# Attention block on one core: low parts of the queries among zeros in full-height tiles, second half of the values behind the convolution's projections, layer norm one step later

## The chip, the cores and the metric

The kernel runs on one core of a Trainium2 chip. A core has a matrix engine (TensorE, PE in the profile, whose weight loads are shown apart as PEld), three engines for elementwise work (VectorE, DVE; ScalarE, ACT; GpSimd, POOL) and a queue engine that issues most transfers (SyncE, SP). Each engine takes its instructions in the order in which they are written for it and waits on semaphores for the others. The metric is the device time of one execution in microseconds.

## The reference, cut to what matters

The program is two transformer blocks, one behind the other. The change lies in the first block, in its attention and convolution branches:

```python
z = rms_norm(x) @ w_in                      # convolution, queries, keys, values, gates
a, gate = split(u)                          # convolution branch
y = a * sigmoid(gate)
y = depthwise_conv(y, 31 taps) + dw_b       # over 1024 tokens
y = silu(layer_norm(y))
# attention branch: 4 heads, two components of 64 features each
s = einsum("bqhcd,bkhcd->bhcqk", q, k) * 64 ** -0.5
p = softmax(where(causal, s, -inf))
a = p[:, :, 0] - lam * p[:, :, 1]           # lam: one number, from four rows of 64
o = rms_norm(einsum("bhqk,bkhe->bqhe", a, v)) * (1 - lam_init)
merged = gates[0] * (conv_out @ w_conv) + gates[1] * (o @ w_attn)
```

A mixture of experts and the second block follow; nothing in them is changed.

## The kernel before

There are 1024 tokens, 1024 features and 128 partitions, so 8 token tiles and 8 feature blocks. Every product of float32 operands is made of three: each operand is split into a high and a low part (`split`, lines 83 to 89: ScalarE makes the high part on L85, VectorE or GpSimd the low one on L86), and `mm3` (L118 to L120) adds high by high, high by low and low by high. `K.weng` names the engine of L86 for weights; during the convolution's projections and the first gates it is GpSimd. Weights come through three buffers for what is loaded and three pairs for what is split.

`phase_a` runs in this order on TensorE: the values, in two halves of 256 columns (each half: 8 token tiles of 24 products, 128x256, into the PSUM tiles PT, copied out by ScalarE on L326); `lambda_a` (the number `lam`: four tiny loads, L275, L276, an Exp on L277, a product on L281) and `consts_b`; the convolution's projections, 8 pairs of 24 + 24 products 128x512 into the banks PB, joined on VectorE on L343; 16 blocks of `gates(0)`, 24 products each; then the queries and keys in eight groups of 96 products 128x256 into PT.

The 31 taps of the convolution (L346, L348) are 124 VectorE instructions over 1024 tokens. They are given a low priority, and the scheduler puts them among VectorE's other work, in the order in which their inputs come; no other large work stands between them.

Each group of queries and keys is normed (ScalarE square, VectorE L428, L132, GpSimd L133, VectorE L431 into `qn`) and turned by transposes one group later (`flip`: `q_T` on L403, `k_T` on L411, whose results VectorE and ScalarE write on L414 and L415). Among the groups stand four steps of the layer norm of the convolution, set by the list `steps`: `ln_mean` (sums over channels on TensorE, L368, then GpSimd and ScalarE) and `ln_rest` (sums of squares on L376, the square root, the gain, the silu).

In the attention loop each of 8 token tiles has 4 heads, and each head two components. A component's scores are made of two products per 512 keys: L472 has the query's high part twice, above itself, against the keys' high and low parts (128 rows of the array), and L473 the query's low part against the keys' high part (64 rows). L475 adds the mask. VectorE takes the maximum (L477), ScalarE the exponential (L480), VectorE joins the components (L488), TensorE transposes (L494), ScalarE copies (L495), TensorE multiplies with the values (L497). `q_parts` (L451 to L453) prepares the parts of two heads. The score tiles are PT, two of them. Into the attention's waits the scheduler puts the products of the other half of the gates (`gates(1)`, L118 to L120 into PB).

Of the kernel before, what the change touches and what calls it, by code (L numbers as in the profile page):

```python
# [19 lines left out]
P = 128  # L20
T = 1024
# [4 lines left out]
CB = 96  # tokens of an expert in a block  # L26
# [8 lines left out]
class Ring:  # L35
    """Buffers taken in turn."""
# [21 lines left out]
def arena(K, pool):  # L58
    """SBUF: slots of [128, 1024], each a line of tiles that follow one another."""

    def new(i, dt=F32):
        return pool.tile([P, 1024], dt, name=nm(f"s{i}"), tag=f"slot{i}")

    K.N = lambda *ii: [new(i) for i in ii]
    K.NR = lambda *ii: [new(i, F32R) for i in ii]
    K.NP = lambda *pp: Ring([(new(a, F32R), new(b, F32R)) for a, b in pp])
# [14 lines left out]
def split(K, src, hi, lo, scale=None, eng=None):  # L81
    """hi + lo = src * scale, both exact in float32r."""
# [9 lines left out]
def split4(K, src, dst):  # L92
    """src [4, 512]: high parts on rows 0 to 3 of dst, low parts on rows 32 to 35, zeros between."""
# [17 lines left out]
def wunit(K, src, kt, n):  # L111
    """src [kt*128, n], loaded and split: views [128, kt, n]."""
    return wsplit(K, wload(K, src, kt, n), kt, n)
# [9 lines left out]
def fm_block(K, u, ps, rh, rl, kt=KD):  # L123
    """Feature-major product: weights stationary, tokens moving."""
# [4 lines left out]
def rstd_pool(K, out, ss, n, scale, eps):  # L129
    """out = (ss * scale + eps) ** -0.5 on [128, n]."""  # L130
# [5 lines left out]
def sig(K, out, src, scale=0.5, bias=None):  # L136
    """sigmoid through tanh, which shares a table with exp."""
# [25 lines left out]
def load_rows(K, specs, buf, ps, engs):  # L163
    """specs: list of (key, AP [r, 128]); per-partition columns: K.cols[key] = AP [128, r]. Returns the step past the loads."""
# [27 lines left out]
def bcast(ap, n, p=P):  # L192
    """A row of n elements in DRAM, on p partitions."""
# [3 lines left out]
def row_rstd(K, x, junk, tag):  # L197
    """(mean square + eps) ** -0.5 of the rows of a token tile."""
# [12 lines left out]
def grow(K, slot, ap, eng=None):  # L211
    """A gain over the features, on all partitions."""
# [5 lines left out]
def norm(K, x, xn, junk, g, tag):  # L218
    """Rms norm of a token tile times g."""
# [11 lines left out]
def turn(K, xn, his, los, j, banks):  # L231
    """A token tile, transposed, split: into tile j of his, los (4 slots each: pairs of feature blocks, 512 tokens)."""
# [34 lines left out]
def lambda_a(K, I, buf):  # L267
    """lambda, and half the gain of the heads' norms with its factor."""
# [19 lines left out]
def phase_a(K, I, gd, cvd, on_out, on_x2):  # L288
# [29 lines left out]
    # values, on tokens  # L318
    V = [kn(s, 2) for s in N(28, 29, 30, 31)]
    rows_a(K, I)  # L320
    for n in range(2):
        us = us if n == 0 else tm_units(2048 + n * 256)
# [4 lines left out]

    lambda_a(K, I, tr())
    consts_b(K, I, tr())

    # convolution branch: gated projections (doubled; the taps are halved), then the taps
# [18 lines left out]
    def gates(q, banks):  # L350
        """Of half the tokens, to DRAM; less 1, doubled: the branches are halved."""
# [7 lines left out]

    gates(0, dn)  # L360
    # layer norm of the convolution over channels, twice its silu: in steps among the queries and keys
# [24 lines left out]
    steps = [[(ln_mean, 0)], [], [(ln_rest, 0)], [(ln_mean, 1)], [], [(ln_rest, 1)], [], []]  # L386

    # queries and keys: on tokens, normed, transposed; the scale goes with the queries.
    # q, a tile pair a slot: [component, head * 128 + token]. A component of the keys of a head has
    # a slot of its own, high and low parts above one another (the high part at the component's rows).  # L390
# [49 lines left out]
    # attention; its normed output, transposed: a tile pair a slot  # L440
    oT = N(0, 1, 2, 3)
    qdr = Ring((46, 47))

    def q_parts(i, hp):
        """Of a pair of heads: the high part of a component twice above itself; the low parts."""
        q = qT[i // 2][:, i % 2 * 512 + hp * 256 : i % 2 * 512 + (hp + 1) * 256]
        qd = NR(qdr())[0]
        ql = qd[:, 512:768]
        for c in range(2):
            r, o, h = comp[c], comp[1 - c], qd[:, c * 256 : (c + 1) * 256]  # L450
            nc.scalar.activation(h[r], q[r], AF.Copy)  # L451
            nc.scalar.activation(h[o], q[r], AF.Copy)
            nc.vector.tensor_tensor(ql[r], q[r], h[r].bitcast(F32), op=ALU.subtract)  # L453
        return qd, ql
# [3 lines left out]
    for i in range(NT):  # L458
        nk = (i + 1) * P
        r0 = K.small.tile([P, 4], F32, name=nm("r0"), tag="r0")  # L460
        for h in range(4):
            if h % 2 == 0:
                qd, ql = q_parts(i, h // 2)
# [1683 lines left out]
```

## Time and profile before

| | |
|---|---|
| runs | 3045.42 us median of 3 (3037.07 to 3050.23) |
| profiled execution | span 3048.1 us; the page gives no other time for it |
| PE busy | 2885.1 us, 95% |
| DVE, ACT, POOL busy | 1941.2, 1361.3, 388.6 us |
| 261.5 to 291.5 us | PE busy 3.63 of 30.00 us |
| 426.5 to 603.6 us (attention) | PE busy 175.85 of 177.10 us |

The stretch that the change touches is the first 605 us or so of the span. A time of the page is counted from the span's start. A busy PE is not a PE at its peak: the matmuls are pipelined, and how fast it goes is read from the distance between the starts of two of them.

### The profile page before, as it was taken

Reading aid. Unit: us, or ns where it says so; the run is one execution under the profiler, and the core shown is the slowest. Engines: PE = TensorE matmul, PEld = TensorE weight load, DVE = VectorE, ACT = ScalarE, POOL = GpSimd, SP = SyncE. Lnnn points to the kernel's source line nnn. Section 1 sums busy time; section 2 is a strip of 40 time slices with the busy share of each in tenths; the row PEclk is TensorE's granted clock in tenths of the full one; section 3 lists DMA queues with packets and bytes.
Section 4 is the critical chain, followed back from the end, with each engine's and each line's share of the span. In section 5 each row is a group of like instructions: output and inputs, shape, how many; then the busy total and the mean of one; then the engine's idle time right before and its main releaser. Section 6 shows DMA issues by size and latency. Waiting matters only on the chain.

```text
span 3048.1 us, 41828 instructions
## 1 busy us (share of the span) xinstructions
PE 2885.1 (95%) x15803; PEld 2287.3 (75%) x15803; DVE 1941.2 (64%) x3245; ACT 1361.3 (45%) x2274; POOL 388.6 (13%) x288
## 2 busy tenths in 40 slices
PE   8996999999979999899799999999899999999998
PEld 7875866787767777777576766777677788888886
DVE  3798476645779998789663554435755565555555
ACT  4121466622458887677432335213456433242222
POOL 2252410000021110110231222210100000000000
PEclk9997989999989999999889989889899999999999
DMA  4141111276589999899741423214343342353332
GB/s 130 48 127 54 35 39 42 80 231 198 203 293 378 372 368 333 300 376 365 247 134 53 113 68 88 68 55 142 106 109 89 95 131 90 97 165 96 92 104 97
DMA packets 365226, 473.29 MB, mean 155 GB/s; under 512 B 36744, under 2 KB 224661, under 8 KB 365020
## 3 DMA queue, kind: packets, MB, share of 16 engines
q1 hardware_dynamic: 357708, 453.26, 45.3%
q0 software_dynamic: 7168, 16.79, 1.7%
q8 instruction: 125, 2.05, 0.3%
q14 instruction: 81, 0.66, 0.1%
q10 hardware_dynamic: 144, 0.52, 0.1%
HBM read 420.65 MB, written 59.02 MB: 157 GB/s over the span
## 4 chain that ended last, share of the span: by engine, by line
PE 44%; DVE 4%; DMA 1%; POOL 1%; ACT 1%; issue 1%; SPq 0%; POOLq 0%; DVEq 0%; ACTq 0%
PE PC L118 11%; PE PC L119 11%; PE PC L120 11%; PE PC L1335 1%; PE PC L1778 1%; PE PC L1442 1%; PE PC L1295 1%; PE PC L1441 1%; PE PC L1772 1%; DMA s<-y2d 0%; PE PC L1424 0%; PE PC L1752 0%; PE PC L1422 0%; PE PC L237 0%; PE PC L1662 0%
## 5 line engine op out<-in xcount | busy, mean ns | idle before, releaser
L85 ACT ACTIVATE s<-s 128x1024 fp32r<-128x1024 f32 (+2 forms) x748 | 716.1, 990 | 719.0 <-PE PC L119 165.8
L86 DVE TENSOR_TENSOR s<-s,s 128x1024 fp32r<-128x1024 f32 (+2 forms) x680 | 750.2, 1137 | 281.3 <-ACT s L85 275.3
L118 PE MATMUL PC<-s,s 128*128 128x512 f32 (+1 forms) x1584 | 635.7, 404 | 0.6 <-ACT s L85 0.4
L119 PE MATMUL PC<-s,s 128*128 128x512 f32 (+1 forms) x1584 | 635.8, 402 | 0.0
L120 PE MATMUL PC<-s,s 128*128 128x512 f32 (+1 forms) x1584 | 634.1, 402 | 1.4 <-DVE s L86 1.4
L118 PE MATMUL PB<-s,s 128*128 128x512 f32 x896 | 355.4, 401 | 13.1 <-ACT s L85 7.7
L119 PE MATMUL PB<-s,s 128*128 128x512 f32 x896 | 356.8, 398 | 0.0
L118 PEld LDWEIGHTS PC<-s,s 128*128 128x128 f32 x1584 | 303.4, 192 | 70.9 <-ACT s L85 6.1
L120 PEld LDWEIGHTS PC<-s,s 128*128 128x128 f32 x1584 | 303.2, 192 | 67.5 <-DVE s L86 4.5
L119 PEld LDWEIGHTS PC<-s,s 128*128 128x128 f32 x1584 | 303.7, 192 | 66.8 <-issue 3.6
L120 PE MATMUL PB<-s,s 128*128 128x512 f32 x896 | 351.5, 397 | 0.0
L119 PE MATMUL PT<-s,s 128*128 128x512 f32 (+1 forms) x896 | 315.2, 352 | 8.3 <-DVE s L86 5.5
L118 PE MATMUL PT<-s,s 128*128 128x512 f32 (+1 forms) x896 | 316.6, 353 | 2.1 <-ACT s L85 2.0
L120 PE MATMUL PT<-s,s 128*128 128x512 f32 (+1 forms) x896 | 312.3, 349 | 0.0
L86 POOL TENSOR_TENSOR s<-s,s 128x1024 fp32r<-128x1024 f32 (+1 forms) x68 | 175.0, 2576 | 401.1 <-ACT s L85 349.7
L118 PEld LDWEIGHTS PB<-s,s 128*128 128x128 f32 x896 | 170.4, 190 | 52.2 <-ACT s L85 11.7
L119 PEld LDWEIGHTS PT<-s,s 128*128 128x128 f32 x896 | 172.0, 192 | 35.7 <-DVE s L86 12.1
L120 PEld LDWEIGHTS PB<-s,s 128*128 128x128 f32 x896 | 170.3, 190 | 34.3
L119 PEld LDWEIGHTS PB<-s,s 128*128 128x128 f32 x896 | 170.3, 190 | 33.5 <-DVE s L86 0.8
L118 PEld LDWEIGHTS PT<-s,s 128*128 128x128 f32 x896 | 172.0, 192 | 24.6 <-ACT s L85 4.1
L348 DVE SCALAR_TENSOR_TENSOR s<-s,convdw,s 128x1011 f32<-128x1011 f32 (+27 forms) x120 | 186.8, 1607 | 1.1
L120 PEld LDWEIGHTS PT<-s,s 128*128 128x128 f32 x896 | 171.7, 192 | 19.3
(511 smaller groups left out, 3325.3 us busy)
## 6 DMA issues: line engine op xcount, KB each, us to landing
s<-in_w_gate_e_dram SPq DMA_DIRECT2D x128, 512.0 KB
s<-in_w_up_e_dram SPq DMA_DIRECT2D x128, 512.0 KB
s<-in_w_down_e_dram SPq DMA_DIRECT2D x128, 512.0 KB
s<-in_w_in_dram SPq DMA_DIRECT2D x90, 512.0 KB
s<-in_ffn_w_up_dram SPq DMA_DIRECT2D x88, 512.0 KB
s<-in_ffn_w_down_dram SPq DMA_DIRECT2D x40, 512.0 KB
s<-in_w_out_dram SPq DMA_DIRECT2D x20, 512.0 KB
s<-in_x_dram SPq DMA_DIRECT2D x16, 512.0 KB
```

Of the source, the lines that this page charges most:

```text
L85: nc.scalar.activation(hi, src, AF.Copy)
L86: (eng or nc.vector).tensor_tensor(lo, src, hi.bitcast(F32), op=ALU.subtract)
L118: nc.tensor.matmul(out, lh, rh, start=start, stop=False)
L119: nc.tensor.matmul(out, lh, rl, start=False, stop=False)
L120: nc.tensor.matmul(out, ll, rh, start=False, stop=stop)
L348: nc.vector.scalar_tensor_tensor(ca[m][:, s:], y[:, : T - s], w[:, 30 - s : 31 - s], ca[m][:, s:], op0=ALU.mult, op1=ALU.add)
L1295: nc.tensor.matmul(pm[:, b * 256 + m * P : b * 256 + m * P + P], BKs[b][fp, j, bo : bo + 2, :].rearrange("p a t -> p (a t)"), ARs[b][fp, j ...
L1335: nc.tensor.matmul(ps[bs : bs + 64, o + h * 64 : o + h * 64 + 64], lhsT[bs : bs + 64, h, :], rv, start=True, stop=True)
L1441: nc.tensor.matmul(yo(h, m), GT[fp, h // 2, m, :], S[fp, h // 2, :], start=True, stop=False)
L1442: nc.tensor.matmul(yo(h, m), M4[h % 2][:, h // 2, m, 64:128], WV[:, h, m, :], start=S is None, stop=True)
L1772: nc.tensor.transpose(pt[:, tile_(t - j0)], p[:, tile_(t)], K.ident)
L1778: nc.tensor.matmul(po[64 * a : 64 * a + 64, tile_(j)], foxv[t // 4][:, t % 4, (2 * hp + a) * 64 : (2 * hp + a + 1) * 64], pTs[a][:, tile_( ...
```

## The change

The values' second half is computed after the convolution's projections, with `lambda_a` and `consts_b` behind it, ahead of `gates(0)`. The steps of the layer norm each move one group later. In the attention, the low parts of the two components get 256 columns each in a tile of 128 partitions; the other 64 partitions are filled with zeros once, by four fills on GpSimd, and the two tiles are kept for the whole loop. L473 then takes 128 rows on either side. The remaining differences are comments taken out (lines behind the first of them have other numbers).

```diff
-    for n in range(2):
-        us = us if n == 0 else tm_units(2048 + n * 256)
+    def values(n, us):
         for i in range(NT):
             ps = pair()[:, :256]
             tm_mm(ps, us, i)
             nc.scalar.activation(V[i // 2][:, i % 2, n * 256 : n * 256 + 256], ps, AF.Copy)

-    lambda_a(K, I, tr())
-    consts_b(K, I, tr())
+    values(0, us)
...
+    values(1, tm_units(2048 + 256))
+    lambda_a(K, I, tr())
+    consts_b(K, I, tr())
     gates(0, dn)
...
-    steps = [[(ln_mean, 0)], [], [(ln_rest, 0)], [(ln_mean, 1)], [], [(ln_rest, 1)], [], []]
+    steps = [[], [(ln_mean, 0)], [], [(ln_rest, 0)], [(ln_mean, 1)], [], [(ln_rest, 1)], []]
...
-    qdr = Ring((46, 47))
+    qds = NR(46, 47)
+    qdr = Ring(qds)
+    for t in qds:
+        for c in range(2):
+            nc.gpsimd.memset(t[comp[1 - c], 512 + c * 256 : 768 + c * 256].bitcast(F32), 0.0)
...
-        qd = NR(qdr())[0]
-        ql = qd[:, 512:768]
+        qd = qdr()
         for c in range(2):
-            r, o, h = comp[c], comp[1 - c], qd[:, c * 256 : (c + 1) * 256]
+            r, o, h, l = comp[c], comp[1 - c], qd[:, c * 256 : (c + 1) * 256], qd[:, 512 + c * 256 : 768 + c * 256]
             nc.scalar.activation(h[r], q[r], AF.Copy)
             nc.scalar.activation(h[o], q[r], AF.Copy)
-            nc.vector.tensor_tensor(ql[r], q[r], h[r].bitcast(F32), op=ALU.subtract)
+            nc.vector.tensor_tensor(l[r], q[r], h[r].bitcast(F32), op=ALU.subtract)
...
-                    nc.tensor.matmul(s[:, n0:m1], ql[comp[c], a : a + P], kc[comp[c], n0:m1], start=False, stop=not last)
+                    nc.tensor.matmul(s[:, n0:m1], qd[:, 512 + c * 256 + a : 512 + c * 256 + a + P], kc[:, n0:m1], start=False, stop=not last)
```

On TensorE, between the first and the second group of queries, this stood before. PT_72 and PT_73 are the groups' sums, s_64 to s_67 the four channel blocks behind the taps:

```order
L120 MATMUL PT_72<-s_34_132,s_9_107 128x256
L368 MATMUL PB_74<-s_64_799,ones 128x512
L368 MATMUL PB_74<-s_65_800,ones 128x512
L368 MATMUL PB_74<-s_66_801,ones 128x512
L368 MATMUL PB_74<-s_67_802,ones 128x512
L118 MATMUL PT_73<-s_32_130,s_10_108 128x256
```

After the change the second group follows the first without a break, and this stands between the second and the third. L405 is the transposes of the first group's queries (L403 before), s_83_1832 its `qn`, and L370 is the former L368:

```order
L120 MATMUL PT_73<-s_34_132,s_17_115 128x256
L405 MATMUL PB_76<-ident,s_83_1832 128x128 x4
L405 MATMUL PB_77<-ident,s_83_1832 128x128 x4
L370 MATMUL PB_74<-s_64_555,ones 128x512
L370 MATMUL PB_74<-s_65_556,ones 128x512
L370 MATMUL PB_74<-s_66_557,ones 128x512
L370 MATMUL PB_74<-s_67_558,ones 128x512
L118 MATMUL PT_72<-s_30_128,s_2_100 128x256
```

So 96 products have moved ahead of the first sums over the taps' results, and the transposes are now the first of the two to need VectorE.

On ScalarE, `lambda_a`'s Exp stood among the splits of the input before, ahead of the values' copies:

```order
L85 ACTIVATE s_10_108<-PB_76 128x2x128
L85 ACTIVATE s_12_110<-PB_77 128x2x128
L277 ACTIVATE lam_761<-lam_761 1x2
L85 ACTIVATE s_11_109<-PB_76 128x2x128
L85 ACTIVATE s_13_111<-PB_77 128x2x128
L326 ACTIVATE s_55_328<-PT_72 128x256
```

After the change it stands behind the last gate of the convolution (L341, L342 before) and ahead of the split of a weight and of all copies of the values' second half:

```order
L341 ACTIVATE s_26_124<-PB_76 128x512
L277 ACTIVATE lam_1317<-lam_1317 1x2
L85 ACTIVATE s_30_128<-s_27_125 128x1024
L326 ACTIVATE s_53_326<-PT_72 128x256
L326 ACTIVATE s_53_326<-PT_73 128x256
L326 ACTIVATE s_54_327<-PT_72 128x256
```

So eight copies that release PT now wait for the input of one small Exp, which comes from VectorE (L276), where it stands among the taps.

On TensorE, behind the eighth group of queries and keys, the last transposes (of s_85_1834, on L411 before and L413 now) stand among the first scores and products of the other gates. Before, of the stretch ahead of them:

```order
L411 MATMUL PB_77<-ident,s_83_1832 128x128 x4
L472 MATMUL PT_72<-s_74_1823,s_114_2879 128x256
L473 MATMUL PT_72<-s_74_1823,s_114_2879 128x256
...
L118 MATMUL PB_75<-s_10_108,s_315_4120 128x512
...
L472 MATMUL PT_73<-s_75_1824,s_114_2879 128x256
L473 MATMUL PT_73<-s_75_1824,s_114_2879 128x256
...
L411 MATMUL PB_76<-ident,s_85_1834 128x128 x4
```

and after the change, with L479 for L472 and L480 for L473:

```order
L413 MATMUL PB_77<-ident,s_83_1832 128x128 x4
L118 MATMUL PB_75<-s_10_108,s_301_4110 128x512
...
L479 MATMUL PT_72<-s_74_1823,s_106_2871 128x256
L480 MATMUL PT_72<-s_74_1823,s_106_2871 128x256
...
L479 MATMUL PT_73<-s_75_1824,s_106_2871 128x256
...
L413 MATMUL PB_76<-ident,s_85_1834 128x128 x4
```

The gates' products ahead of the last transposes are 19 before and 22 after; 13 of these now stand ahead of the first score, where none stood.

## Rows read from the trace of the kernel before

**Rows 1.** Windows: length, busy us (instructions) of PE, PEld, DVE, ACT, POOL; clock, DMA.

```profile
249.50:261.50 12.00, 12.00 (x99) 11.79 (x98) 12.00 (x11) 1.71 (x3) 0.00 (x0) 1.00 0.19 64
261.50:291.50 30.00, 3.63 (x7) 0.91 (x5) 29.40 (x25) 0.86 (x1) 0.00 (x0) 0.57 0.00 0
393.30:399.60 6.30, 1.90 (x9) 1.49 (x9) 5.54 (x8) 3.79 (x7) 0.51 (x1) 0.69 0.00 0
412.50:426.50 14.00, 13.69 (x40) 9.85 (x41) 8.11 (x30) 8.46 (x27) 0.00 (x0) 0.51 0.18 57
426.50:603.60 177.10, 175.85 (x920) 124.60 (x919) 121.48 (x251) 115.20 (x249) 8.39 (x8) 1.00 0.17 52
```

**Rows 2.** Waits of PE, 0 to 330 us: total us, times, longest.

```profile
PE PB L368 <- DVE s L348: 26.4, 2, 21.2
PE PB L118 <- DVE s L343: 2.9, 1, 2.9
```

**Rows 3.** Timeline of DVE: start us, duration us, instruction, idle before it.

```profile
35.74 0.27 DVE L276 TENSOR_REDUCE lam<-s 1x2 f32<-1x128 f32 x1
93.50 0.81 DVE L346 TENSOR_SCALAR s<-s,convdw,cols 128x1024 f32<-128x1024 f32 x1
...
291.32 1.22 DVE L86 TENSOR_TENSOR s<-s,s 128x1024 fp32r<-128x1024 f32 x1
296.92 1.23 DVE L431 TENSOR_TENSOR s<-PT,rsq 128x1024 f32<-128x1024 f32 x1 [3.04 <-POOL rsq L133]
```

**Rows 4.** Taps beside weight splits: line L348, one pair in time, POOL from 93.5 to 291.

```profile
L348 DVE SCALAR_TENSOR_TENSOR s<-s,convdw,s x120: 1239/1264/3472, 94.3 to 290.2; 128x1023 f32<-128x1023 f32 x4, 128x1022 f32<-128x1022 f32 x4, 128x1021 f32<-128x1021 f32 x4, 128x1020 f32<-128x1020 f32 x4
...
137.21 3.43 DVE L348 SCALAR_TENSOR_TENSOR s<-s,convdw,s 128x1001 f32<-128x1001 f32 x1
...
137.19 2.39 POOL L86 TENSOR_TENSOR s<-s,s 128x1024 fp32r<-128x1024 f32 x1 [2.15 <-ACT s L85]
...
L86 POOL TENSOR_TENSOR s<-s,s 128x1024 fp32r<-128x1024 f32 x22 | 66.2, 3012 | 91.4 <-ACT s L85 91.4
```

**Rows 5.** Timeline of PE around the first sums over the taps' results.

```profile
291.46 2.08 PE L368 MATMUL PB<-s,ones 128*128 128x512 f32 x2 [21.18 <-DVE s L348]
...
306.30 1.03 PE L403 MATMUL PB<-ident,s 128*128 128x128 f32 x8
```

**Rows 6.** Timeline of ACT: a copy of the values' second half.

```profile
53.14 0.39 ACT L326 ACTIVATE s<-PT 128x256 f32<-128x256 f32 x1 [2.50 <-PE PT L120]
```

**Rows 7.** Timelines of SP and POOL: a small load and who waited for it.

```profile
35.23 0.43 SPq L1004 DMA_DIRECT2D relb<-in_rel_bias_dram  x1
...
38.18 0.16 POOL L605 IOTA s<- 128x16 int32 x1 [4.58 <-DMA relb<-in_rel_bias_dram]
```

**Rows 8.** Timeline of PE in the attention: scores, mask, gates' products.

```profile
533.13 0.50 PE L473 MATMUL PT<-s,s 64*128 64x512 f32 x1
533.56 0.44 PE L472 MATMUL PT<-s,s 128*128 128x384 f32 x1
533.92 0.45 PE L473 MATMUL PT<-s,s 64*128 64x384 f32 x1
534.30 0.23 PE L475 MATMUL PT<-maskb,identb 128*128 128x128 bf16 x1
...
534.89 0.39 PE L120 MATMUL PB<-s,s 128*128 128x512 f32 x1
535.12 0.39 PE L118 MATMUL PB<-s,s 128*128 128x512 f32 x1
```

**Rows 9.** Groups by line, 0 to 850 us: count, busy us, mean ns, idle before.

```profile
L473 PE MATMUL PT<-s,s 64*128 64x512 f32 (+2 forms) x96 | 44.2, 460 | 0.0
L805 POOL MEMSET s<- 128x1024 f32 x3 | 2.8, 960 | 11.8 <-PE PB L119 11.8
```

**Rows 10.** Waits of the other engines, 410 to 625 us.

```profile
ACT s L495 <- PE PB L494: 27.1, 33, 2.0
DVE mx L477 <- PE PT L475: 22.5, 29, 2.3
```

More of the change, by code (lines that the diff above doesn't have):

```diff
@@ L441, in phase_a @@
     oT = N(0, 1, 2, 3)
-    qdr = Ring((46, 47))
+    qds = NR(46, 47)
[3 more added lines that the diff above has]
+            nc.gpsimd.memset(t[comp[1 - c], 512 + c * 256 : 768 + c * 256].bitcast(F32), 0.0)
     def q_parts(i, hp):
         q = qT[i // 2][:, i % 2 * 512 + hp * 256 : i % 2 * 512 + (hp + 1) * 256]
-        qd = NR(qdr())[0]
-        ql = qd[:, 512:768]
+        qd = qdr()
         for c in range(2):
-            r, o, h = comp[c], comp[1 - c], qd[:, c * 256 : (c + 1) * 256]
+            r, o, h, l = comp[c], comp[1 - c], qd[:, c * 256 : (c + 1) * 256], qd[:, 512 + c * 256 : 768 + c * 256]
             nc.scalar.activation(h[r], q[r], AF.Copy)
             nc.scalar.activation(h[o], q[r], AF.Copy)
-            nc.vector.tensor_tensor(ql[r], q[r], h[r].bitcast(F32), op=ALU.subtract)
-        return qd, ql
+            nc.vector.tensor_tensor(l[r], q[r], h[r].bitcast(F32), op=ALU.subtract)
+        return qd
     sr, ptr, po = Ring(PT), Ring(PB[0:1]), PB[2]
@@ L462, in phase_a @@
             if h % 2 == 0:
-                qd, ql = q_parts(i, h // 2)
+                qd = q_parts(i, h // 2)
             ps_, sms = [], []
```

## The prediction

> **What bounds the kernel now.** I read the slices of the page first. The matrix engine is busy nearly everywhere, so a gain must come from the stretches in which it waits, or in which a busy engine moves slowly. The windows find them [rows 1]. From 249.5 to 261.5 us PE is full at the granted clock 1.00. From 261.5 to 291.5 it works 3.63 of 30 us. At 393.3 to 399.6 it works 1.90 of 6.3 us. From 412.5 to 426.5 it counts as busy, but at 0.51 of the clock, the lower of its two levels (1.2 GHz). From 426.5 to 603.6, in the attention, PE is busy 175.85 of 177.1 us, while VectorE has 121.5 us of work and ScalarE 115.2.
>
> The waits name who holds the first hole: 26.4 us for the last results of the taps [rows 2]. VectorE's timeline shows the length of that chain: the run of taps begins with L346 at 93.50 and is over at 291.32, 197.8 us without a break [rows 3]. So this place is bound by VectorE and not by the matrix engine, and it ends when the run ends. The attention is bound by PE: VectorE waits 22.5 us there for scores and ScalarE 27.1 us for transposes [rows 10], and these are engines with a third of their time free.
>
> **The change part by part.**
>
> *The order of values and convolution.* The values' second half is 8 tiles, one copy every 0.39 + 2.50 = 2.9 us [rows 6], so 8 x 2.88 = 23 us. The products do not change in number. The convolution starts 23 us earlier, and so do the taps: 93.5 - 23.0 = 70.5 us. The run then ends 23 us earlier as well, at 268.3, unless it grows. It grows by three things. First, weight splits on GpSimd. A tap takes 1.26 us in the median, but the one that meets a split at 137.2 takes 3.43, which is 2.2 us more [rows 4]. Before, 22 such splits lie in the run [rows 4]; the two of the values' second half, which were over before it began, now lie in it too: 2 x 2.2 = 4.4 us. Second, `lambda_a` and `consts_b` now put eight small instructions among the taps, of up to 0.27 us each like L276 [rows 3]: some 1.5 us. Third, L275 needs its four loads, and these can be issued only when the convolution's seventh gate has given up the buffer. The nearest small load came 38.18 - 35.23 = 2.95 us behind its issue [rows 7]; the loads are issued one behind the other, 0.43 us apart, and two taps and an L346 cover most of this. I take 2 us. The run ends at about 276.
>
> What follows it is the same chain as before: split, sum, power, then L431, from 291.32 to 296.92 + 1.23 = 298.15 [rows 3], 6.8 us. The first transposes can go at 283. Then they (1.03 us warm [rows 5], double that at the lower clock) and four sums of 1.04 us each (2.08 for two, [rows 5]) stand ahead of the third group: it begins at about 289. Before it began at 307.1, right behind the transposes of 306.30 [rows 5]. That is **18 us**; for a restart at the lower clock I take 1 off: **17**. Without any growth it would be 24; if the loads, the Exp or the splits cost another 8 us, 9.
>
> *The wait that this adds.* L277 stands on ScalarE in front of all copies of the values' second half, and it waits for L276, which stands among the taps. The last gate of the convolution is ready some 23 us earlier than before; the seventh of VectorE's joins (L343) is late by then, because taps stand ahead of it: before, the eighth one cost PE 2.9 us in this way [rows 2]. TensorE can fill the two tiles of PT, 5.8 us, and must then wait for a copy. Ahead of L276 VectorE has, by the new order, 45 taps, 3 L346, 5 joins, and by then 6 splits get in: 45 x 1.2 + 3 x 0.8 + 5 x 0.7 + 6 x 2.2 = 73 us from 70.5, and with 2 us for the loads it comes near 146. The values' second half begins when the last six pairs are done, 6 x 48 products of 0.23 us [rows 8] behind 70: about 136. So L276 is some 10 us late, a split of 1 us on ScalarE stands ahead of the first copy too, and with 5.8 us covered PE waits 5 to 8 us, near 142; I take 8. I cost this at nothing, for this reason: the second group of queries ends at 261.5 + 11.6 - 2.9 + 8 = 278 (a group of 96 is 12.00 x 96/99 = 11.6 us, [rows 1]; the wait of 2.9 us goes, as 23 us of values now stand between the joins and the gates that need their banks). The transposes cannot go before 283, so 5 us are left over. If that cover is gone, each further us is lost. The next thing late is still the run of taps: about 5 us of idle time remain at the first transposes in place of 26.4.
>
> *The steps of the layer norm.* They are not fewer. The first step loses its wait to the transposes ahead of it. The last `ln_rest` moves behind the seventh group, and its work on VectorE, ScalarE and GpSimd now stands ahead of the last group's norm rather than the one before. So the hole of 6.3 us at 393.3 [rows 1] moves to the last transposes, behind which only the first scores stand. 22 of the gates' products stand ahead of them now, 19 before: 3 x 0.23 = 0.7 us more cover. PE will wait longer at one place, and less at the other. I take 0, with 5 us either way; the clock belongs in here, as a long hole can bring the level of 0.51 [rows 1] behind it, or move it.
>
> *Full height.* Scores alternate between 128 rows (L472) and 64 (L473). From start to start: L473 to L472 0.43 us and L472 (384 columns) to L473 0.36, L473 to the mask 0.38, but between two gates' products of 512 columns, both of 128 rows, 0.23 us [rows 8]. Three quarters of that, 0.17, would be 384 columns. So a 64-row product costs 0.19 us when entered and 0.20 when left. The first score of a head can stand behind a short transpose, which hides part; I take 0.36 for a pair of changes. There are 96 such products [rows 9]: 96 x 0.36 = 35 us. They then have 128 rows like all others, with the same columns.
>
> The Trainium skill, page "TensorEngine Tiling (Array Packing)", section "Key Properties", says that changing the tiling mode drains the TensorE; the steps agree. But the page "TensorE: Matmul & The Clock Gate", sections "Step-by-step: what each phase is for" and "Why this matters for your kernels", says that time goes by columns, the row count doesn't matter, and that a product of 32 rows takes as long as one of 128; by that rule alone this edit gives 0.
>
> Not all 35 us arrive. In 426.5 to 603.6 lie 86 of the 96 products, so PE's part falls to 177 - 31 = 146 us, against 121.5 on VectorE, 83%. VectorE's idle time there falls from 56 to 25 us, under 1 us for each of 28 heads, and a head is a chain (maximum, exponential, join, transposes, copy) through three engines. I take three quarters: **26 us**. Ends: 10 (PE soon waits for this chain) and 35 (all of it).
>
> *The fills.* Four on GpSimd, of 64x256; the nearest row, 128x1024, is 0.96 us [rows 9]. GpSimd has 8 us of work in the whole attention [rows 1]; behind them waits only the last norm's power, which needs VectorE's later sum anyway: 0. Uncovered they would cost 2 us.
>
> **The sum**: 17 + 0 + 26 + 0 = 43 us. Against the profile's span: 3048.1 - 43 = 3005. The median of the runs is 2.7 us below that span, and the page gives nothing else around it; the predicted median is 3045.4 - 43 = **3002**.
>
> **Rivals.**
>
> *A, the attention gives little.* Either height sets no time, as the rule above has it, or VectorE and ScalarE take over as soon as PE is faster. For: 83% on VectorE. Against: the steps of 0.43 and 0.23, and 50 us of waiting for PE [rows 10]. With 0 to 10 us of the 35: 3045 - 17 - 5 = 3023.
>
> *B, the run of taps ends later.* L276 or the loads come late, PE's wait near 142 outgrows its 5 us of cover, or the splits cost more. Then 7 us instead of 17: 3012.
>
> *C, slower: the clock.* With fewer products of the gates among the first heads and one longer hole ahead of them, PE stays at the lower level into the attention. At that level a product takes twice its time; from 412.5 to 426.5 it shows how a stretch looks in which PE has work [rows 1]. Of the 146 us left in the attention, 43 us done at the lower level would eat all that is won; half of them, 73 us, gives 3002 + 73 = 3075. Against: the level came back within 14 us, and held for 177.
>
> *D, the change moves the wait only.* The hole is as long at the transposes as at the sums, and the attention's gain is eaten at its start: 3040.
>
> **How the numbers follow.** My forecast, with either main term inside its bounds: 0.66. A 0.16, B 0.10, C 0.04, D 0.04. The low end is all terms at their best, 17 + 7 for taps without growth, 35, 5: 64; that they come together is unlikely, so I take 62: 2983. The high end takes in A at its worse end and B's middle: 9 + 8 = 17 us won, 3028. Some 0.5% (15 us) is what a measurement of this kernel can tell from no change. Faster by more, under 3030: the forecast, B and most of A, 0.90. Within: a rest of A, and D, 0.06. Slower: C, 0.04.
>
> **What would show it.** The run of taps ends at 274 to 279 and the third group begins near 289; PE waits some 8 us near 142 for L326, and some 5 us for the first transposes, none of it for the taps' sums. In the attention every step between products of 512 columns is near 0.23 us, and the time from the eighth group's end to the last transposes of the attention's output falls from 210 to some 184 us. I'm wrong if the run of taps ends where it did, if PE shows new waits for L488, L480 or L495 that sum to more than 20 us, or if the windows of the attention show a clock well under 1.00.

## The result

| kernel | median of its runs | span of the profiled execution |
|---|---|---|
| before | 3045.28 us (4 runs, 3037.07 to 3050.23) | 3048.1 us |
| changed | 3007.81 us (4 runs, 2998.58 to 3012.77) | 3011.0 us |

The ratio is 0.9854, with an interval of 0.9831 to 0.9878. A second measurement with nothing edited ("again", below) gave 0.9841, 0.9816 to 0.9866. The forecast of 3002 us was 6 us low, and its range held the time.

### The profile page after: what moved, and what is told of

Same layout as the page of the kernel before. It is cut to its first block, busy times and chain, and to the rows that moved or that the text cites. A ratio compares the mean times of both kernels' runs of the same rounds, so it can differ in the third digit from the quotient of the medians.

```text
span 3011.0 us, 41833 instructions
## 1 busy us (share of the span) xinstructions
PE 2864.9 (95%) x15803; PEld 2289.9 (76%) x15803; DVE 1939.0 (64%) x3245; ACT 1357.5 (45%) x2274; POOL 403.1 (13%) x292
## 4 chain that ended last, share of the span: by engine, by line
PE 45%; DVE 4%; POOL 1%; DMA 1%; ACT 1%; issue 1%; SPq 0%; POOLq 0%; DVEq 0%; ACTq 0%
PE PC L119 11%; PE PC L118 11%; PE PC L120 11%; PE PC L1342 1%; PE PC L1785 1%; PE PC L1302 1%; PE PC L1449 1%; PE PC L1448 1%; PE PC L1779 1%; DMA s<-y2d 1%; PE PC L1431 0%; PE PC L1759 0%; PE PC L237 0%; PE PC L1429 0%; DVE s L223 0%
## 5 line engine op out<-in xcount | busy, mean ns | idle before, releaser
L86 POOL TENSOR_TENSOR s<-s,s 128x1024 fp32r<-128x1024 f32 (+1 forms) x68 | 188.3, 2771 | 401.4 <-ACT s L85 351.4
L118 PEld LDWEIGHTS PB<-s,s 128*128 128x128 f32 x896 | 170.1, 190 | 47.8 <-ACT s L85 10.8
L347 DVE SCALAR_TENSOR_TENSOR s<-s,convdw,s 128x1001 f32<-128x1001 f32 (+23 forms) x120 | 194.5, 1670 | 1.0
```

The costliest lines, as they stand in the source:

```text
L86: (eng or nc.vector).tensor_tensor(lo, src, hi.bitcast(F32), op=ALU.subtract)
L118: nc.tensor.matmul(out, lh, rh, start=start, stop=False)
L347: nc.vector.scalar_tensor_tensor(ca[m][:, s:], y[:, : T - s], w[:, 30 - s : 31 - s], ca[m][:, s:], op0=ALU.mult, op1=ALU.add)
```

## The profile after

First the windows of the changed kernel, with the columns of [rows 1]:

```profile
249.50:279.60 30.10, 30.10 (x229) 29.01 (x228) 26.44 (x21) 5.82 (x7) 5.40 (x2) 1.00 0.22 71
...
372.30:378.60 6.30, 0.10 (x2) 0.08 (x1) 6.06 (x10) 4.75 (x9) 2.22 (x4) 0.91 0.00 0
378.60:385.50 6.90, 6.46 (x21) 4.55 (x21) 4.22 (x7) 4.73 (x9) 3.15 (x2) 0.59 0.00 1
385.50:397.00 11.50, 7.37 (x32) 5.68 (x32) 8.80 (x28) 9.77 (x29) 0.00 (x0) 0.74 0.07 24
397.00:555.20 158.20, 154.38 (x922) 122.09 (x922) 123.89 (x264) 113.18 (x257) 8.45 (x8) 1.00 0.20 61
```

The empty stretch of 30 us is gone: from 249.5 us up to the first transposes TensorE is full at clock 1.00. A hole of 6.3 us now stands ahead of the first score, with 18 us at 0.59 and 0.74 behind it. In the rest of the attention TensorE is busy 154.38 of 158.2 us, at 1.00.

Of the waits of TensorE from 0 to 330 us and from 366 to 560 us, the two longest behind the start of the program in each (total us, times, longest):

```profile
PE PB L120 <- POOL s L86: 3.8, 1, 3.8
PE PT L118 <- ACT s L326: 2.8, 1, 2.8
...
PE PT L479 <- ACT s L459: 6.2, 1, 6.2
PE PT L479 <- ACT s L487: 3.9, 6, 1.3
```

No wait names the taps any more, where [rows 2] has 26.4 us. The timelines of VectorE and of TensorE show how closely it fits (L345 opens the run of taps, L405 is the first transposes, L370 the sums):

```profile
70.03 0.81 DVE L345 TENSOR_SCALAR s<-s,convdw,cols 128x1024 f32<-128x1024 f32 x1
...
271.75 1.22 DVE L86 TENSOR_TENSOR s<-s,s 128x1024 fp32r<-128x1024 f32 x1
...
277.36 1.23 DVE L433 TENSOR_TENSOR s<-PT,rsq 128x1024 f32<-128x1024 f32 x1 [3.05 <-POOL rsq L133]
...
278.64 0.28 PE L120 MATMUL PT<-s,s 128*128 128x256 f32 x1
278.77 1.03 PE L405 MATMUL PB<-ident,s 128*128 128x128 f32 x8
279.64 3.60 PE L370 MATMUL PB<-s,ones 128*128 128x512 f32 x8
282.67 0.68 PE L118 MATMUL PT<-s,s 128*128 128x256 f32 x1
```

What the transposes need is ready at 277.36 + 1.23 = 278.59, and TensorE starts its last product ahead of them at 278.64. The run of taps is 201.7 us long, 3.9 more than in [rows 3].

In the attention, the weight loads of score products show where the time of [rows 8] went. Ahead are three of the kernel before, then three of the changed one with their products:

```profile
533.13 0.18 PEld L473 LDWEIGHTS PT<-s,s 64*128 64x128 f32 x1 [0.25 <-issue]
533.55 0.19 PEld L472 LDWEIGHTS PT<-s,s 128*128 128x128 f32 x1 [0.24 <-issue]
533.92 0.18 PEld L473 LDWEIGHTS PT<-s,s 64*128 64x128 f32 x1 [0.18 <-issue]
...
514.36 0.19 PEld L480 LDWEIGHTS PT<-s,s 128*128 128x128 f32 x1
514.47 0.19 PEld L479 LDWEIGHTS PT<-s,s 128*128 128x128 f32 x1
514.70 0.19 PEld L480 LDWEIGHTS PT<-s,s 128*128 128x128 f32 x1
...
514.39 0.48 PE L480 MATMUL PT<-s,s 128*128 128x512 f32 x1
514.70 0.34 PE L479 MATMUL PT<-s,s 128*128 128x384 f32 x1
514.88 0.34 PE L480 MATMUL PT<-s,s 128*128 128x384 f32 x1
```

Before, each load begins only when its own product does (533.13 stands in both timelines), behind an idle time that nothing the profile shows explains. After, L479's load begins at 514.47, under the product that started at 514.39. From L479 to L480 it takes 514.88 - 514.70 = 0.18 us for 384 columns, where [rows 8] gives 0.36.

To compare kernels with different line numbers, I use one product of the constants behind the first attention block (L1019 before, L1026 after), which stands ahead of the experts:

```profile
L1019 PE MATMUL PT<-s,relb x2: 482/482/482, 719.1 to 719.4; 33*4 33x383 f32 x2
...
L1026 PE MATMUL PT<-s,relb x2: 482/482/482, 674.8 to 675.1; 33*4 33x383 f32 x2
```

At this **mark** the changed kernel is 719.1 - 674.8 = 44.3 us ahead, 1 us more than the forecast sum. The span is only 37 us shorter: 7 us net are given back in the second block, whose code is the same. Its windows show where most of it goes, those of the kernel before first (the same instructions in each pair):

```profile
1603.80:1628.50 24.70, 23.42 (x259) 17.09 (x261) 11.34 (x30) 6.20 (x15) 3.12 (x3) 0.93 0.12 34
1641.50:1666.70 25.20, 25.16 (x293) 18.95 (x292) 8.81 (x28) 4.70 (x13) 2.06 (x4) 1.00 0.16 41
...
1558.50:1585.90 27.40, 27.36 (x258) 20.50 (x260) 9.40 (x30) 6.16 (x15) 2.86 (x3) 0.75 0.10 30
1598.90:1628.10 29.20, 29.20 (x293) 22.25 (x292) 9.19 (x28) 4.77 (x13) 2.07 (x4) 0.82 0.14 36
```

These two stretches cost 2.7 and 4.0 us more, at a granted clock of 0.75 and 0.82 in place of 0.93 and 1.00. Of the kernel before there is one profile only. In twelve of the thirteen other ones the lead shrinks between 1500 and 1800 us, by 3 to 24 us, so it may be the 0.93 and 1.00 that are the exception.

## The experiments

All were timed against the kernel before, in five rounds. "Ahead" is the distance at the mark, read from one profile. The mark contains what the clock did ahead of it, and the ratio, which is of the times, what it did later too.

| run | mark, us | ahead, us | ratio of the time, interval |
|---|---|---|---|
| the changed kernel | 674.8 | 44.3 | 0.9854, 0.9831 to 0.9878 |
| again | 674.6 | 44.5 | 0.9841, 0.9816 to 0.9866 |
| old_steps | 669.9 | 49.2 | 0.9839, 0.9815 to 0.9863 |
| early_steps | 670.2 | 48.9 | 0.9825, 0.9800 to 0.9850 |
| early_lambda | 691.5 | 27.6 | 0.9907, 0.9883 to 0.9932 |
| height_only | 691.3 | 27.8 | 0.9940, 0.9920 to 0.9961 |
| order_only | 697.3 | 21.8 | 0.9938, 0.9911 to 0.9966 |
| dve_splits | 664.0 | 55.1 | 0.9804, 0.9774 to 0.9834 |
| lambda_breaks | 689.5 | 29.6 | 0.9899, 0.9868 to 0.9930 |
| best | 657.0 | 62.1 | 0.9798, 0.9774 to 0.9823 |
| before_dve_splits | 690.2 | 28.9 | 0.9911, 0.9889 to 0.9934 |
| grouped | 706.7 | 12.4 | 0.9965, 0.9942 to 0.9988 |
| dve_height | 665.8 | 53.3 | 0.9854, 0.9822 to 0.9887 |

**again.** No edit.

> The changed kernel once more, nothing edited. In its profile the second block's stretch from 1558.5 to 1628.1 us, whose code the change does not touch, ran at granted clocks of 0.75 and 0.82 where the kernel before had 0.93 and 1.00, and some 10 us of the gain were lost between there and 1780 us. Theory (the clock there differs from one execution to the next): up to 820 us this profile agrees with the first one within 1.5 us, and the second block's loss differs by 5 us or more; the median comes at 3000 to 3012 us. Rival (the change moves the second block into a bad place each time): the same two stretches show 0.75 and 0.82 again, and the gain at the end is again 8 to 10 us smaller than at 1550 us.

The first 720 us repeat within 0.4 us. The stretches from 1558.5 and 1598.9 us show 0.75 and 0.82 again, as the rival said; but the end came at a span of 3005.5, some 5 us earlier, since from 1776 to 1998 us the clock was 0.96 and 0.92 where the first profile had 0.93 and 0.89 in the same work. So neither held alone: part of the loss comes back with the same kernel, part differs between executions.

**old_steps.**

```diff
-    steps = [[], [(ln_mean, 0)], [], [(ln_rest, 0)], [(ln_mean, 1)], [], [(ln_rest, 1)], []]
+    steps = [[(ln_mean, 0)], [], [(ln_rest, 0)], [(ln_mean, 1)], [], [(ln_rest, 1)], [], []]
```

> The changed kernel with the layer norm's steps one group earlier, as they stood before the change. Theory (the move of the steps is worth about nothing): the first sums wait again for the taps, some 5 us at 267 us, so the third group begins some 5 us later than in the changed kernel; in exchange the hole of 6.2 us ahead of the first score shrinks by 2 to 6 us. Together -3 to +4 us against the changed kernel. Rival (the move is what won the 4 us by which the eighth group ended earlier than forecast, and the tail does not care): 5 to 9 us slower than the changed kernel.

At the mark it is 4.9 us ahead of the changed kernel, just outside the theory and on the side opposite to the rival's. The first sums wait 1.8 us for the taps, not 5. The last transposes of the attention's output end at the same time in both; but 281 of the other gates' products lie ahead of them, and 257 in the changed kernel. One block of 24, at 0.23 us each, has been pushed behind the attention. These products are no added work, so they stand for time that TensorE lost ahead of them. From the eighth group's end to the last transposes, the changed kernel first:

```profile
368.50:555.20 186.70, 172.10 (x994) 135.34 (x993) 146.07 (x308) 133.19 (x302) 17.62 (x17) 0.96 0.17 53
...
371.90:555.20 183.30, 173.90 (x1019) 136.91 (x1019) 142.45 (x304) 131.15 (x296) 12.68 (x11) 0.98 0.19 57
```

The changed kernel is idle there for 14.6 us, old_steps for 9.4, and its mean clock is lower; in exchange its eighth group ends 3.4 us earlier. The times (0.9839 here, 0.9841 in again) don't show the 4.9 us.

**early_steps.**

```diff
-    steps = [[], [(ln_mean, 0)], [], [(ln_rest, 0)], [(ln_mean, 1)], [], [(ln_rest, 1)], []]
+    steps = [[], [(ln_mean, 0)], [(ln_rest, 0)], [(ln_mean, 1)], [(ln_rest, 1)], [], [], []]
```

> The changed kernel with the later steps of the layer norm moved up: sums behind the second and the fourth group, the rest behind the third and the fifth, nothing behind the last three. Theory (the hole of 6.2 us ahead of the first score and the lower clock of 0.59 and 0.74 behind it come from the last step's work on VectorE and ScalarE, which stands ahead of the last group's norm and of the first query parts): the hole falls to 2 to 3 us, the stretch up to 397 us loses some 3 us of its low clock, 6 to 9 us faster than the changed kernel, near 3000 us. Rival (the hole is the last group's own chain of square, sum, power and transposes): within 2 us of the changed kernel, the hole still above 5 us.

4.6 us ahead of the changed kernel at the mark, again with 281 products, and the wait ahead of the first score is 2.7 us. The cause is the theory's, the hole and the lower clock behind it; its size was put too high.

**early_lambda.**

```diff
     values(0, us)
+    lambda_a(K, I, tr())
+    consts_b(K, I, tr())
...
     values(1, tm_units(2048 + 256))
-    lambda_a(K, I, tr())
-    consts_b(K, I, tr())
```

> The changed kernel with the small number lambda and the constants computed behind the first half of the values, ahead of the convolution, so that no Exp waits among the taps. Theory (the wait of 2.8 us near 142 us is covered): the wait goes, but TensorE then stands some 2 us at the first transposes, since these wait for the run of taps; the run itself ends 1 to 2 us earlier, as eight small instructions and a wait for their loads are gone from it: 1 to 2 us faster than the changed kernel, no more. Rival (nothing covers it): the whole 2.8 us and the wait of 3.8 us near 169 go, 5 to 7 us faster.

It is 16.7 us behind the changed kernel at the mark, which neither theory allowed. The wait at 142 us is gone; the one at 169 us has grown from 3.8 to 20.3. Its wait, the split on GpSimd, and VectorE beside it (L349 is the taps, L347 the opening of the next channel block):

```profile
PE PB L120 <- POOL s L86: 20.3, 1, 20.3
...
162.29 26.42 POOL L86 TENSOR_TENSOR s<-s,s 128x1024 fp32r<-128x1024 f32 x1 [18.23 <-ACT s L85]
...
153.43 33.07 DVE L349 SCALAR_TENSOR_TENSOR s<-s,convdw,s 128x1007 f32<-128x1007 f32 x28
186.43 2.82 DVE L347 TENSOR_SCALAR s<-s,convdw,cols 128x1024 f32<-128x1024 f32 x1
```

GpSimd began at 162.29 and was kept out through 21 taps, until VectorE came to an instruction that is no tap; that one took 2.82 us instead of 0.81 [rows 3]. In the changed kernel the same split met `lambda_a`'s copy of `lam` (L283), seven taps on:

```profile
162.62 10.38 POOL L86 TENSOR_TENSOR s<-s,s 128x1024 fp32r<-128x1024 f32 x1 [11.73 <-ACT s L85]
...
158.92 11.87 DVE L347 SCALAR_TENSOR_TENSOR s<-s,convdw,s 128x1018 f32<-128x1018 f32 x10
170.72 0.15 DVE L283 COPY lam<-PB 128x1 f32<-128x1 f32 x1
170.78 14.37 DVE L347 SCALAR_TENSOR_TENSOR s<-s,convdw,s 128x1013 f32<-128x1013 f32 x5
```

So that copy among the taps, which I had counted as a small cost, ended a wait at 3.8 us.

**lambda_breaks.** The kernel of early_lambda with this in the taps' loop:

```diff
             for s in range(1, 31):
+                if s % 4 == 0:
+                    nc.vector.tensor_scalar(brk, ca[m][:, T - 1 :], 1.0, None, op0=ALU.mult)
```

> The kernel of early_lambda (20 us slower than the changed one, with a wait of 20.3 us at 168 us for a split on GpSimd that took 26.4 us beside 21 taps) with one tiny VectorE instruction, a copy of one column that nothing reads, behind every fourth tap. Theory (GpSimd is kept out while VectorE goes from tap to tap, and let in at the first instruction that is no tap): the split takes 3 to 9 us, the wait falls from 20.3 to under 6 us, and the kernel is 10 to 16 us faster than early_lambda although 28 instructions of about 0.1 us were added. Rival (the split is slow for another reason, its input or its queue): the wait stays above 15 us.

```profile
162.38 2.88 POOL L86 TENSOR_TENSOR s<-s,s 128x1024 fp32r<-128x1024 f32 x1 [18.25 <-ACT s L85]
...
PE PB L408 <- DVE s L436: 18.9, 1, 18.9
```

The split takes 2.88 us and the wait at 168 us is gone, as the theory has it; but it was let in at the next tap and not at one of the tiny instructions, so how these help is open. And only 2 us are won, for the wait turns up as 18.9 us at the first transposes (L408). The run of taps now ends at 284.7 instead of 275.6 us. TensorE's 20 us at 168 had hidden that run's lateness: whoever takes a wait away here meets the taps next.

**dve_splits.** The changed kernel, with the weights' splits on VectorE through the convolution and the first gates:

```diff
-    K.weng = nc.gpsimd
+    K.weng = None
```

> The changed kernel with the low parts of the weights made on VectorE instead of GpSimd during the convolution and the first gates. Theory (a split on GpSimd costs the tap that meets it 2.2 us, on VectorE it takes 1.2, and GpSimd can wait many taps until it is let in): the 24 splits of the run cost 24 x 1.0 = 24 us less, the run of taps ends near 250 instead of 272 us, the wait of 3.8 us at 169 goes, and TensorE, now without a wait for the taps, is some 4 to 7 us earlier at the third group; 4 to 7 us faster than the changed kernel. Rival (VectorE's splits come late behind the taps in its queue): TensorE waits for L86 on VectorE for more than 5 us in sum, no faster or slower.

```profile
71.87 1.28 DVE L347 SCALAR_TENSOR_TENSOR s<-s,convdw,s 128x1023 f32<-128x1023 f32 x1
...
250.53 1.22 DVE L86 TENSOR_TENSOR s<-s,s 128x1024 fp32r<-128x1024 f32 x1
251.66 1.25 DVE L347 SCALAR_TENSOR_TENSOR s<-s,convdw,s 128x994 f32<-128x994 f32 x1
...
267.93 1.04 PE L405 MATMUL PB<-ident,s 128*128 128x128 f32 x8
```

The run ends at 252.9, 19 us earlier, and both waits of TensorE in the run are gone. The first transposes start at 267.93 instead of 278.77, 10.8 us earlier: 6.6 for the two waits, and most of the rest because the clock stays at 1.00 from 130 to 200 us, where the waits had left 0.94 and 0.96. The run's end and the end of the wait at 169 us came as the theory has it. The gain is above its 4 to 7 us, and not for its reason, a wait for the taps: the taps are now done 15 us before the transposes start, and what was won are TensorE's own two waits, of which it had named one.

**order_only and height_only.** The changed kernel with the half-height low parts (the core of the edit first), and the kernel before with the full-height ones, its fills and its two kept tiles:

```diff
-                    nc.tensor.matmul(s[:, n0:m1], qd[:, 512 + c * 256 + a : 512 + c * 256 + a + P], kc[:, n0:m1], start=False, stop=not last)
+                    nc.tensor.matmul(s[:, n0:m1], ql[comp[c], a : a + P], kc[comp[c], n0:m1], start=False, stop=not last)
```

```diff
-                    nc.tensor.matmul(s[:, n0:m1], ql[comp[c], a : a + P], kc[comp[c], n0:m1], start=False, stop=not last)
+                    nc.tensor.matmul(s[:, n0:m1], qd[:, 512 + c * 256 + a : 512 + c * 256 + a + P], kc[:, n0:m1], start=False, stop=not last)
```

> The changed kernel with the half-height low parts of before: only the order of values and convolution, with lambda and the constants, and the later steps of the layer norm. Theory (the parts add up; the order is worth 25 us at the eighth group's end and some 5 are given back by the later steps at the attention's start): 17 to 23 us faster than before, the run of taps ends at 272 us, and the attention's pairs of scores stay at 0.43 and 0.36 us. Rival (the two parts overlap, since a faster attention only waits for VectorE): order and height alone sum to 10 us more than both together.

> The kernel before with the full-height low parts alone. Theory (a 64-row product costs 0.19 us when entered and 0.20 when left, and three quarters of it arrive): up to 393 us nothing changes; the attention, from the eighth group's end to the last transposes of its output, falls from 211 to 180 to 186 us; one block of the other gates (24 products, 5.5 us) then has to be done behind it; 20 to 26 us faster than before. Rival A (the height sets no time, or VectorE and ScalarE take over): the attention falls by 10 us or less, 0 to 10 us faster.

Height alone is 27.8 us ahead, above the theory's 20 to 26; no block of gates was pushed out, as the steps stood as before. The attention took 577.2 - 393.9 = 183.3 us in place of 210.8. But not all of this is the height's. Here is the first of the eight token tiles, from the eighth group's end to the last transposes of its output, in before, in before_dve_splits (below; its attention is not edited) and in height_only, and then the seven later tiles in before and in height_only:

```profile
393.30:434.10 40.80, 34.94 (x131) 24.57 (x131) 27.78 (x68) 23.82 (x59) 4.42 (x3) 0.75 0.12 39
369.60:405.90 36.30, 30.67 (x130) 21.74 (x131) 27.64 (x68) 23.60 (x59) 4.36 (x3) 0.86 0.14 44
393.90:427.50 33.60, 26.38 (x130) 19.69 (x131) 27.51 (x67) 22.98 (x60) 4.90 (x4) 0.90 0.15 48
...
434.10:604.10 170.00, 168.75 (x888) 119.86 (x888) 116.64 (x237) 110.05 (x237) 7.38 (x7) 1.00 0.17 54
427.50:577.20 149.70, 147.47 (x889) 117.22 (x888) 114.98 (x238) 108.10 (x237) 7.75 (x7) 1.00 0.19 60
```

With the same products the first tile takes 40.8 us at a mean clock of 0.75 and 36.3 at 0.86. So of height_only's 7.2 us there, some 4.5 are the clock's. In the later tiles, at 1.00, the height is worth 170.0 - 149.7 = 20.3 us, 0.23 for each of their 88 products. Together at most 20.3 + 36.3 - 33.6 = 23.0 us are the height's, inside the theory's range.

Order alone is 21.8 ahead: 24.2 at the eighth group's end, of which 4.0 are given back by the end of the attention, as its theory has it; the run of taps ends at 272.4. The two sum to 49.6, and together they give 44.3. The 5.3 us show at the mark as the 24 gates' products left over behind the attention, which neither part alone leaves there (284 and 281 lie inside). Most of the time that they stand for was lost in the first tile: it takes 38.2 us at a clock of 0.82 with 44 of them, in height_only 33.6 at 0.90 with 56. VectorE didn't take over: the seven later tiles take 148.5 us, with 12 of these products fewer than in height_only's 149.7. In the times height_only is 18 us faster, less than its mark says; its profile loses 12 us between 1577 and 1654 us, at a clock of 0.76.

**grouped.** The kernel before, with the scores in another order:

```diff
                 for n0 in range(0, nk, 512):
+                    m1 = max(min(nk, n0 + 512), n0 + 256)
+                    nc.tensor.matmul(s[:, n0:m1], qd[:, c * 256 + a : c * 256 + a + P], kc[:, n0:m1], start=True, stop=False)
+                for n0 in range(0, nk, 512):
                     n1 = min(nk, n0 + 512)
                     last = n1 == nk
                     m1 = max(n1, n0 + 256)
-                    nc.tensor.matmul(s[:, n0:m1], qd[:, c * 256 + a : c * 256 + a + P], kc[:, n0:m1], start=True, stop=False)
```

> The kernel before with the order of a component's scores changed for the four later token tiles, which have two pieces of keys: both products of the high part first, then both half-height ones of the low part. The same products, two changes of height per component instead of four, 64 changes fewer in all. Theory (the cost belongs to the change of height, 0.19 us each): 64 x 0.19 = 12 us less work of TensorE, 9 to 12 us less between 477 and 604 us. Rival (a 64-row product is slower in itself): no more than 2 us.

12.4 us ahead at the mark, for 64 changes of height fewer. Over 64 that would be 0.19 us each, but 4.3 us of it came in the first token tile, which has no second piece of keys and whose clock was 0.86 in place of 0.75. Where the edit acts, from the third tile's last transposes (the fifth tile's first scores stand at 477 us before) to the eighth's, before and then grouped:

```profile
470.10:604.10 134.00, 132.91 (x709) 94.98 (x708) 89.48 (x169) 84.31 (x173) 5.27 (x5) 1.00 0.17 53
...
467.50:592.00 124.50, 123.12 (x708) 92.19 (x708) 88.84 (x169) 83.40 (x173) 5.27 (x5) 1.00 0.18 56
```

That is 9.5 us, 0.15 for each change: the low end of the theory, and far above the rival's 2. The products with 64 rows were as many as before, so this part of the cost belongs to the change. That their rows cost nothing in themselves is not shown by it.

**before_dve_splits, best, dve_height.** The first is the kernel before with this line; the second the changed kernel with this line and the edit of old_steps; the third the kernel before with this line and the edit of height_only:

```diff
-    K.weng = nc.gpsimd
+    K.weng = None
```

> The kernel before with the low parts of the weights made on VectorE during the convolution and the first gates, and nothing else. Theory (the stretch from 261.5 to 291.5 us ends when the run of taps ends, and each split on GpSimd lengthens it by 1 us more than on VectorE): the run of 197 us becomes 176 to 180 us and ends at 271 to 275, the wait of 26.4 us for the taps' results falls to 6 to 11 us, 15 to 20 us faster than before, without any new order. Rival (the taps are not what sets this place): the wait moves elsewhere, 0 to 5 us faster.

> The changed kernel with the splits of dve_splits and the steps of old_steps together. Theory (they are worth 10.7 and 4.6 us at 719 us of the kernel before and lie at different places): 59 to 61 us ahead of the kernel before at that point, against 44.4 for the changed kernel, no wait of TensorE over 1 us between 14 and 340 us, and 281 instead of 257 of the other gates' products inside the attention; 2985 to 2995 us. Rival (with the taps done early the later steps are as good, and the earlier sums wait): within 2 us of dve_splits at that point.

> The kernel before with two edits only: the splits of the weights on VectorE during the convolution and the first gates, and the full-height low parts. The order of values and convolution, lambda, the constants and the layer norm's steps stay as before. Theory (they lie at different places and add up): 28.1 + 27.8 = 56 us ahead of the kernel before at its 719 us, 281 gates' products inside the attention; so, against the 62.0 us of best, the new order of values and convolution is worth 6 us once the splits are on VectorE, in place of 22. Rival (with the run of taps still later than TensorE, the rest of the order's gain stays): 45 us or less, the order still worth 15 or more.

The line alone is 28.9 us ahead, more than the whole new order and more than the theory's 15 to 20. 23.7 of it stand at the eighth group's end and 4.5 in the first token tile, where only the clock differs. Part of the 23.7 is the scheduler's: it now puts the second group and the first transposes ahead of the last sums, which wait 2.3 us for the taps instead of 26.4; other splits, still on GpSimd, cost 7.7 us of waits. best is 62.1 ahead at the mark, just above its theory's 59 to 61 (one wait of 2.0 us remains), and the fastest median, 2990.24 us against 3050.62 of before, 60 us. Its ratio is not told from that of dve_splits, as the intervals overlap. dve_height comes within 3 us of the theory, which adds the clock's gain in the first token tile twice, as it is in both of its terms. Beside the line and the height, the new order (with the old steps) is worth 62.1 - 53.3 = 8.8 us.

## Why the prediction was right

*The order, forecast 17: right mechanism, mis-sized.* The third group began at 282.7, against 307.1 before: 24.4 us. Two parts were put too high. The run of taps grew by 3.9 us, where I had 4.4 + 1.5 + 2; VectorE did not stand for the loads, and the transposes came 4.2 us before the 283 of the forecast. And I let TensorE restart at the lower clock; it came without an idle moment, so the transposes and four sums took 3.9 us (278.77 to 282.67) and not 6, and the 1 us taken off was not due. 17 + 4.2 + 2.1 + 1 = 24.3.

*The wait near 142: named rightly, 2.8 us and not 8.* L276 came at 142.05 and L277 at 142.35, not 146. That it costs nothing held narrowly: 5 us of idle time were to remain at the first transposes, and 0 remained. The cover went to what I had not seen, the 3.8 us for GpSimd at 169 and the clock of 0.94 and 0.96 behind the two waits.

*The layer norm's steps, forecast 0 with 5 either way: they cost 4.9.* This is the term of the forecast's sum that failed, at the edge of its bound. The hole did move to the attention's start, as said, but it isn't worth the same there: 5.2 us more of idle time and a lower clock, against 3.4 us won ahead of it (old_steps). The fillers show it: I weighed three more of the gates' products at the hole, and over the attention they went down by 24.

*Full height, forecast 26: 27.8 at the mark, at most 23.0 of them the height's.* The mechanism is right, and the size was put a little too high: 0.23 us for each product in the later tiles, where 26 us over 96 are 0.27. The clock in the first tile made up the rest, which is luck. In the changed kernel, eighth group's end (368.5) to the last transposes (555.2) is 186.7 us where 184 was said. The group of half-height products and the waits of VectorE and ScalarE answer to [rows 9, 10]:

```profile
L480 PE MATMUL PT<-s,s 128*128 128x512 f32 (+2 forms) x96 | 34.2, 363 | 0.0
...
DVE mx L484 <- PE PT L482: 5.8, 13, 1.1
ACT s L502 <- PE PB L501: 14.8, 19, 2.5
```

VectorE's wait for scores falls from 22.5 to 5.8 us, but it did not become the bound: rival A is out. Not every step is 0.23: from L479 to L480 it is 0.34 where the score tile came free just in time. The Trainium skill, page "TensorE: Matmul & The Clock Gate", section "Step-by-step: what each phase is for", says of a weight load that the row count doesn't matter. The trace agrees, 0.18 us with 64 rows and 0.19 with 128. What cost time here is the change between row counts, 0.15 us each in grouped.

*The fills, 0:* four took 1.6 us, and the profile shows nobody waiting for them.

*Rivals.* B did not come: the run ended earlier than said. C: the lower clock came at the attention's start, 18 us at a mean of 0.59 and 0.74, and not for the 43 us that would have eaten the gain. D: the hole at the transposes is gone. Of the 44.3 us at the mark the profile keeps 37; the rest went in the second block, most of it beside a lower clock, and what sets that is open.

*The sum.* That 43 stands so near to 44.3 is in part luck: the order gave 7 us more than was put, the steps took 5, and the height itself gave some 3 less. The times can't tell it finer: the medians lie 37.5 us apart in the first measurement and 49.9 in the second. The working of the range's high end, 9 + 8, doesn't fit its own words, since A at its worse end gives 0 and B's order gives 7; the range didn't need it.

## What to carry to other kernels

A long run on one engine can be lengthened by another engine's help: here each split on GpSimd beside a tap cost VectorE 2.2 us, and making it on VectorE itself 1.2. When a wait is taken away, look up which chain it was hiding, and count again what the scheduler moves into or out of the gap. Products of different heights in turn cost by the change, so zeros, or another order, can be cheaper than fewer rows. And compare stretch by stretch: 4 us that seemed to be an edit's came from a tile that it had not touched.

## What was unexpected in the hardware

A GpSimd split beside VectorE's taps was let in at the next tap in most cases, and took 2.4 to 3.5 us. But three of the changed kernel's 24 got in only at the first instruction that was no tap (5.8, 6.5 and 10.4 us), and in early_lambda one took 26.4. The Trainium skill, "SBUF — State Buffer", section "SBUF: two separate sides", says that VectorE's instructions with two SBUF inputs and GpSimd's that read SBUF take a shared port in turn, each for a whole instruction, and the loser waits. The tap of 3.43 us beside a split of 2.39 [rows 4] agrees; a wait through 21 instructions is not in it. What decides between the two was not tried and stays open.
